# Decoder layer with retrieved experts: one sum kept in PSUM through the dense loop, gate loads of two rounds, and the second projection's first steps placed earlier

## The chip, the core and the metric

The kernel runs on one core of one Trainium2 chip. The number that counts is the device time of one execution in microseconds (us). The core has a matrix engine (TensorE, PE in the profile; its weight loads are listed as PEld), three engines for elementwise work (VectorE = DVE, ScalarE = ACT, GpSimd = POOL), and SyncE (SP), which here only starts DMA transfers. GpSimd also starts the indirect transfers that fetch table rows by index.

## What is computed

One decoder layer for 1024 tokens of width 1024, all in float32. The reference, cut to its spine:

```python
x   = layer_norm(x, ln_in)
p   = x @ w_in                          # 3592 columns, split into 8 parts
fox = causal attention, 8 heads x 64, logits + cumulative log forget gate
hgr = gated recurrence, 4 heads, state 128 x 128
x   = layer_norm(ALPHA * x + concat(fox, hgr) @ w_out, ln_mix)
# PEER: every token takes 8 heads x 16 = 128 of 16384 one-neuron experts
q   = x @ w_q
s   = scores of q against 2 x 128 sub-keys per head
idx, gates = top 16 of the pair sums per head, softmax
h   = gelu(x . u_tab[idx]) * gates
x   = layer_norm(ALPHA * x + sum_e h_e * v_tab[idx_e], ln_ffn)
```

## The kernel before

Tokens are worked in eight blocks of 128 and three groups: blocks 0 and 1 (group 0), 2 to 5 (group 1), 6 and 7 (group 2). Float32 products are made of three matmuls in a rounded format (`mm3`): each operand is split into `hi` (a rounded copy, by ScalarE) and `lo` (the rest, by one subtraction on VectorE or GpSimd), and hi·hi, hi·lo and lo·hi are added up in PSUM.

The stages, in the order of emission in `mixers`: input projection of group 0 (`project`, `project_cols`: 17 column tiles `m` of 128 columns, then row-wise parts), the two mixers of group 0 (`fox`, `hgrn`), `mix_out` with a layer norm, `select` (queries, scores, top 16), `select_tail` (pair sums, indices, gates; nearly all VectorE). Then the input projection of the other 768 tokens: `preload` loads their six normalised blocks from DRAM, `project` transposes them (48 transposes into `psf` banks, the hi and lo parts written to `xh`, `xl`; in every second block by a ScalarE copy `tsx` and a subtraction on GpSimd) and `project_cols` does the 17 column tiles at 768 columns. Then groups 1 and 2 follow in the same way without a further projection.

The experts are done in two ways. For blocks 0, 1, 6, 7 (`GATHER`) GpSimd fetches one expert row for each of 128 tokens at a time into one of eight row buffers (`rows`, 128x1024), and VectorE multiplies it with the tokens and sums (`gather_u`, L1124) or adds it, scaled, to the output (`gather_v`, L1149). These steps wait in queues (`ujobs`, `vjobs`) that `tick` draws on while other stages are emitted, by rates of each stage; after group 0, `HOLD = 7` ticks pass before the first. For blocks 2 to 5 (`DENSE`, 512 tokens) all 16384 experts are computed: `gbuild` writes the gates as a dense table `d_g` to DRAM, and `dense` loops over it.

`dense` has 32 rounds of four tiles of 128 experts. `up(g)` loads the round's gates `gt` (1 MB), and for each tile a 512-KB piece of u (`ur`), splits it, makes 24 matmuls into a `psh` bank, then gelu, gate product (L1047) and split. `down(g)` does the 1024 output columns in two halves of 512: per half four tiles of v (`vr`, 256 KB), four token blocks, three matmuls each, into four banks (three `psf`, one `psv`); after the half VectorE adds each bank to the sum `y` in SBUF (L1064, 128x512). PSUM holds two `psh`, one `psv` and three `psf` banks and one tile `y` of two banks (`psy`), which only `gather_v` of block 0 uses. `down` of a round runs beside `up` of the next, and the gather steps of the last blocks run all along. `finish` and `finish_dense` do the last layer norm; its two rows g, b are loaded once, at the start of the dense loop (`lnf`), into two buffers of their own.

Instructions are emitted in this order, and then a scheduler places them on each engine by estimated costs, so that work of a later stage may stand earlier. Every engine runs its own list in order. Nearly all loads are started by SP, in order.

Of the kernel before, what the change touches and what calls it, by code (L numbers as in the profile page):

```python
# [8 lines left out]
F32 = mybir.dt.float32  # L9
# [11 lines left out]
P = 128  # L21
# [18 lines left out]
HOLD = 7  # L40
# [7 lines left out]
GORD = (0, 1, 2, 3, 4, 5)  # L48
Q = {"qk": "a", "hs": "a"}
# [20 lines left out]
JG = 4  # L70


class Layer:
    def __init__(self, ctx, tc, a, out, dbg=None):
# [3 lines left out]
        self.ujobs, self.vjobs, self.bjobs, self.owed = [], [], [], [0.0] * 3  # L78
        self.nu = self.nv = 0
        self.hold = 0.0  # L80
        self.lnf = None
# [94 lines left out]
    def tick(self, phase, T=None, w=1.0):  # L176
        rate = RATE[phase] if T is None else RATE[phase][T]
# [145 lines left out]
    def mixers(self, groups, es):  # L323
        st, gb, tl = ExitStack(), ExitStack(), ExitStack()
# [5 lines left out]
        for n, (t0, T) in enumerate(groups):  # L330
# [32 lines left out]
            if n == 0:  # L363
                x1 = self.preload(T, S - T)
# [10 lines left out]
            if n == 0:  # L375
                x1 = self.project(T, S - T, st, x1)
                self.lx.close()
# [42 lines left out]
    def project(self, t0, T, st, xs=None):  # L420
        pa = st.enter_context(self.pool("pa", 1, "right"))
        xh = pa.tile([P, DC, T], F32R, name="xh", tag="xh")
        xl = pa.tile([P, DC, T], F32R, name="xl", tag="xl")

        def split(n, x):
            self.transpose_split("f", x, xh, xl, n)

        if t0:
            with self.pool("pt", 2, "right") as pt:
                for n, x in enumerate(xs):  # L430
                    self.transpose_split("f", x, xh, xl, n, pt if n % 2 < PSPL else None)
        else:
            pl = self.lx.enter_context(self.pool("pl", 2, "left"))
            self.first_ln(pl, 0, T, split)
            self.lns = [lambda r0=r0: self.first_ln(pl, r0, 2 * P, lambda n, x: None) for r0 in range(T, S, 2 * P)]
        return xh, xl

    def preload(self, t0, T):
        pl = self.lx.enter_context(self.pool("pl", 1, "left"))
        xs = []  # L440
        for n in range(T // P):
            x = pl.tile([P, D], F32, name="x", tag="x", bufs=T // P)
            self.q("x1l").dma_start(x, self.d_x1[t0 + n * P : t0 + (n + 1) * P])
            xs.append(x)
        return xs

    def project_cols(self, t0, T, xh, xl):
# [3 lines left out]
        with self.pool("pb", 2, "right") as pb:  # L451
            for m in range(17):
# [566 lines left out]
    def dense(self, prep, tail, tl):  # L1019
# [4 lines left out]
        with self.pool("dw", 2, "left") as dw, dws:  # L1024
# [9 lines left out]

            def up(g):
                gt = dw.tile([P, TD // 32, JG, 32], F32, name="gt", tag="gt")
                nc.sync.dma_start(gt, self.d_g[:, :, g * JG : (g + 1) * JG, :].rearrange("q j i t -> j q i t"))
                for c in range(JG):
# [8 lines left out]
                    nc.vector.tensor_tensor(h3, h3, gt[:, :, c], op=ALU.mult)  # L1047
# [3 lines left out]

            def down(g, hs):
# [15 lines left out]
            def late():  # L1068
# [3 lines left out]
                self.lnf = self.ffn_rows([dv[0].tile([P, D], F32, name=n, tag=n, bufs=1) for n in ("dlg", "dlb")])  # L1072
# [3 lines left out]
            for g in range(NG + 1):  # L1076
# [21 lines left out]
            self.finish_dense(dv[0], y, dv[1])  # L1098

    def rows(self):  # L1100
        return self.gp.tile([P, D], F32, name="rows", tag="rows", bufs=NROWS)
# [122 lines left out]
    def finish(self, y, r0):  # L1224
# [4 lines left out]
        g, b = self.lnf or self.ffn_rows([self.rows() for _ in range(2)])  # L1229
# [87 lines left out]
```

## Time and profile before

| | us |
|---|---|
| time, median of 3 runs (lowest, highest) | 3052.78 (3049.38, 3057.18) |
| the profiled execution | 3059.49 |
| its span, first to last instruction | 3057.6 |
| mean granted clock of the matrix engine, share of full speed | 0.921 |
| PE busy in the span | 2614.2 (85%) |
| DVE busy | 2667.8 (87%) |
| ACT, POOL busy | 1091.4 (36%), 1612.5 (53%) |
| DMA | 887.11 MB, mean 290 GB/s |

The stages from the span's start: projection of group 0 until 121 us, its mixers until 197, `mix_out` and layer norm until 235, selection until 302, the tail of the selection with the transposes of the other blocks until 346, the 768-column projection until 586, the rest of groups 1 and 2 until 1515, the dense loop until 3037, the last layer norm until the end. A busy share is a mean over stages that differ: which engine sets the time is read stage by stage. Every engine's list is in order, so an instruction that waits also holds all that stand behind it.

### The profile page before, as it was taken

Reading aid. Unit: us, or ns where it says so; the run is one execution under the profiler, and the core shown is the slowest. Engines: PE = TensorE matmul, PEld = TensorE weight load, DVE = VectorE, ACT = ScalarE, POOL = GpSimd, SP = SyncE. Lnnn points to the kernel's source line nnn. Section 1 sums busy time; section 2 is a strip of 40 time slices with the busy share of each in tenths; the row PEclk is TensorE's granted clock in tenths of the full one; section 3 lists DMA queues with packets and bytes.
Section 4 is the critical chain, followed back from the end, with each engine's and each line's share of the span. In section 5 each row is a group of like instructions: output and inputs, shape, how many; then the busy total and the mean of one; then the engine's idle time right before and its main releaser. Section 6 shows DMA issues by size and latency. Waiting matters only on the chain.

```text
span 3057.6 us, 45196 instructions
## 1 busy us (share of the span) xinstructions
PE 2614.2 (85%) x15865; PEld 2140.4 (70%) x15865; DVE 2667.8 (87%) x5555; ACT 1091.4 (36%) x2068; POOL 1612.5 (53%) x1216
## 2 busy tenths in 40 slices
PE   7778699877669768779578999899989999999995
PEld 6768589755567545568457878777768877877874
DVE  8658776588778998689898999899999999999998
ACT  4733222365312233677522323232223323223321
POOL 2344377655665645110156666565476665656652
PEclk9878899878889879889789999999999999999998
DMA  7632499855877867865589999999999999999994
GB/s 278 195 138 90 178 333 326 256 157 163 303 279 270 288 199 255 312 258 194 192 305 343 361 366 381 333 370 368 345 355 363 372 386 362 359 361 342 371 334 164
DMA packets 338660, 887.11 MB, mean 290 GB/s; under 512 B 29912, under 2 KB 124136, under 8 KB 336000
## 3 DMA queue, kind: packets, MB, share of 16 engines
q0 software_dynamic: 147456, 536.94, 48.3%
q1 hardware_dynamic: 185200, 338.38, 31.7%
q10 hardware_dynamic: 5776, 8.90, 0.8%
q8 instruction: 125, 2.05, 0.3%
q14 instruction: 103, 0.84, 0.1%
HBM read 821.67 MB, written 62.42 MB: 289 GB/s over the span
## 4 chain that ended last, share of the span: by engine, by line
PE 40%; DVE 37%; issue 9%; DMA 6%; ACT 4%; POOL 3%; SPq 0%; DVEq 0%; POOLq 0%; ACTq 0%
DVE ys L1149 7%; PE psf L294 6%; PE psf L295 6%; PE psf L293 5%; DVE rows L1124 5%; PE psh L293 5%; PE psh L295 5%; PE psh L294 5%; POOL rows L1105 2%; DMA rows<-in_u,gsel 1%; DVE tw L808 1%; DVE dy L1064 1%; PE psv L294 1%; PE psv L718 1%; PE psv L295 1%
## 5 line engine op out<-in xcount | busy, mean ns | idle before, releaser
L1105 POOL DMA_INDIRECT rows<-in_u,gsel x512 | 688.4, 1345 | 585.6 <-DVE rows L1124 368.8
L1105 POOL DMA_INDIRECT rows<-in_v,gsel x512 | 640.9, 1252 | 437.7 <-DVE ys L1149 271.2
L1124 DVE SCALAR_TENSOR_TENSOR rows<-rows,gx 128x1024 f32<-128x1024 f32 x512 | 635.6, 1291 | 36.6 <-DMA rows<-in_u,gsel 27.8
L1149 DVE SCALAR_TENSOR_TENSOR ys<-rows,sd,ys 128x1024 f32<-128x1024 f32 x381 | 491.2, 1289 | 0.6
L293 PE MATMUL psh<-dxh,uh 128*128 128x512 f32 x1024 | 403.0, 394 | 29.4 <-ACT uh L1031 16.6
L295 PE MATMUL psh<-dxh,ul 128*128 128x512 f32 x1024 | 401.1, 392 | 9.5 <-DVE ul L1032 9.4
L294 PE MATMUL psh<-dxl,uh 128*128 128x512 f32 x1024 | 400.6, 391 | 0.0
L294 PE MATMUL psf<-vl,hh 128*128 128x512 f32 x768 | 311.0, 405 | 42.2 <-DVE vl L1032 41.4
L1031 ACT ACTIVATE vh<-vr 128x512 fp32r<-128x512 f32 x256 | 161.8, 632 | 436.1 <-PE psv L295 396.1
L295 PE MATMUL psf<-vh,hl 128*128 128x512 f32 x768 | 306.4, 399 | 0.0
L293 PE MATMUL psf<-vh,hh 128*128 128x512 f32 x768 | 278.5, 395 | 10.7 <-DVE dy L1064 8.8
L1031 ACT ACTIVATE uh<-ur 128x1024 fp32r<-128x1024 f32 x128 | 135.8, 1062 | 405.1 <-PE psh L294 400.0
L293 PEld LDWEIGHTS psh<-dxh,uh 128*128 128x128 f32 x1024 | 193.6, 189 | 77.2 <-ACT hs L1045 20.4
L295 PEld LDWEIGHTS psh<-dxh,ul 128*128 128x128 f32 x1024 | 193.5, 189 | 50.4 <-DVE ul L1032 10.5
L294 PEld LDWEIGHTS psh<-dxl,uh 128*128 128x128 f32 x1024 | 193.5, 189 | 39.5
L294 PEld LDWEIGHTS psf<-vl,hh 128*128 128x128 f32 x768 | 148.1, 193 | 89.7 <-DVE vl L1032 59.0
L215 ACT ACTIVATE whi<-wraw 128x1024 fp32r<-128x1024 f32 x106 | 111.6, 1056 | 230.9 <-PE psf L294 64.8
L1032 DVE TENSOR_TENSOR vl<-vr,vh 128x512 fp32r<-128x512 f32 x256 | 170.7, 689 | 12.0 <-ACT vh L1031 11.9
L293 PEld LDWEIGHTS psf<-vh,hh 128*128 128x128 f32 x768 | 145.5, 190 | 48.1 <-DVE dy L1064 9.8
L218 DVE TENSOR_TENSOR wlo<-wraw,whi 128x1024 fp32r<-128x1024 f32 x60 | 81.8, 1365 | 100.8 <-ACT whi L215 98.0
L295 PEld LDWEIGHTS psf<-vh,hl 128*128 128x128 f32 x768 | 148.1, 193 | 29.8
L1032 DVE TENSOR_TENSOR ul<-ur,uh 128x1024 fp32r<-128x1024 f32 x128 | 156.6, 1224 | 11.5 <-ACT uh L1031 10.5
(342 smaller groups left out, 6156.5 us busy)
## 6 DMA issues: line engine op xcount, KB each, us to landing
ur<-in_ut SPq DMA_DIRECT2D x128, 512.0 KB
vr<-in_v SPq DMA_DIRECT2D x256, 256.0 KB
d_g<-slab SPq DMA_DIRECT2D x16, 2048.0 KB
gt<-d_g SPq DMA_DIRECT2D x32, 1024.0 KB
wraw<-in_wq SPq DMA_DIRECT2D x48, 512.0 KB
wraw<-in_wt SPq DMA_DIRECT2D x34, 512.0 KB
wraw<-in_wn SPq DMA_DIRECT2D x24, 512.0 KB
wraw<-in_wo SPq DMA_DIRECT2D x24, 512.0 KB
```

Source lines behind the costliest of these rows:

```text
L215: nc.scalar.activation(hi, raw, AF.Copy)
L218: eng.tensor_tensor(lo, raw, hi.bitcast(F32), op=ALU.subtract)
L293: mm(out, lh, rh, start=start, stop=False, **kw)
L294: mm(out, lh, rl, start=False, stop=False, **kw)
L295: mm(out, ll, rh, start=False, stop=stop, **kw)
L718: nc.tensor.matmul(pv[:, qb], ps[:, qb * P : (qb + 1) * P], V[:, kb], start=kb == 0, stop=kb == b0 + qb, skip_group_check=True)
L808: nc.vector.match_replace(w, out_v[:, 0:8], vals, FMIN)
L1031: nc.scalar.activation(hi, raw, AF.Copy)
L1032: nc.vector.tensor_tensor(lo, raw, hi.bitcast(F32), op=ALU.subtract)
L1105: self.nc.gpsimd.indirect_dma_start(out=t, out_offset=None, in_=tab, in_offset=bass.IndirectOffsetOnAxis(ap=idx, axis=0))
L1124: self.pin(nc.vector.scalar_tensor_tensor(u, u, 1.0, x2, op0=ALU.mult, op1=ALU.mult, accum_out=sd[:, n : n + 1]), "u")
L1149: self.pin(nc.vector.scalar_tensor_tensor(ys, v, h, ys, op0=ALU.mult, op1=ALU.add), "w")
```

## The change

Five parts. `down` keeps the sum of dense block 0 (`tb = 0`, token block 2) in the two banks of the `psy` tile through all 32 rounds, and adds it to `y` once, in the last; the other three blocks take `psf`, `psf`, `psf` in the first half and `psv`, `psf`, `psf` in the second. The gates of two rounds come with one load (`GT = 8`). `early` takes the place of `preload` and of the transposes in `project`: it is a sequence of steps that `tick` calls during the attention of group 0 (0.34 of a step at each of 18 ticks); six steps load and transpose one block each, into the `psy` tile, with ScalarE copies and VectorE subtractions; four more do the first four column tiles (`NEARLY = 4`) with raw, hi and lo in three of the `rows` buffers and the product in the `psy` tile; what is left is drained before `select_tail`. `project_cols` then begins at `m = 4`. `HOLD` becomes 3.5. And `lnf` is gone: each `finish` loads g and b into two `rows` buffers, `finish_dense` takes two `ur` buffers.

```diff
-HOLD = 7
+HOLD = 3.5
+NEARLY = 4
+ERATE = {"fox": 0.34, "hgrn": 0.0, "mix": 0.0, "sel": 0.0}
+GT = 8
...
     def tick(self, phase, T=None, w=1.0):
+        if self.ahead and phase in ERATE:
+            self.due += w * ERATE[phase]
+            while self.due >= 1.0:
+                self.due -= 1.0
+                next(self.ahead, None)
+            return
...
+            if n == 0:
+                pa = ex.enter_context(self.pool("pa", 1, "right"))
+                x1 = [pa.tile([P, DC, S - T], F32R, name=m, tag=m) for m in ("xh", "xl")]
+                self.ahead = self.early(T, S - T, *x1, pa)
...
-            if n == 0:
-                x1 = self.preload(T, S - T)
...
             if n == 0:
-                x1 = self.project(T, S - T, st, x1)
-                self.lx.close()
+                self.drain([self.ahead])
+                self.ahead = None
...
+    def early(self, t0, T, xh, xl, pa):
+        nc, a = self.nc, self.a
         for n in range(T // P):
+            x = self.rows()
             self.q("x1l").dma_start(x, self.d_x1[t0 + n * P : t0 + (n + 1) * P])
+            pt = self.psy.tile([P, D], F32, name="y", tag="y")
+            for c in range(DC):
+                nc.tensor.transpose(pt[:, c * P : (c + 1) * P], x[:, c * P : (c + 1) * P], self.ident)
+            sl = slice(n * P, (n + 1) * P)
+            for c0 in range(0, DC, 4):
+                v = pt[:, c0 * P : (c0 + 4) * P].rearrange("p (c t) -> p c t", c=4)
+                h = xh[:, c0 : c0 + 4, sl]
+                nc.scalar.activation(h, v, AF.Copy)
+                nc.vector.tensor_tensor(xl[:, c0 : c0 + 4, sl], v, h.bitcast(F32), op=ALU.subtract)
+            yield
+        for m in range(NEARLY):
+            raw, hi, lo = self.rows(), self.rows(F32R), self.rows(F32R)
+            self.q("w").dma_start(raw, a["wt"][m])
+            nc.scalar.activation(hi, raw, AF.Copy)
+            nc.vector.tensor_tensor(lo, raw, hi.bitcast(F32), op=ALU.subtract)
+            wh, wl = (t.rearrange("p (c m) -> p c m", c=DC) for t in (hi, lo))
+            po = self.psy.tile([P, D], F32, name="y", tag="y")
+            s = pa.tile([P, T], F32, name="es", tag="es", bufs=1)
+            for c0 in range(0, T, 512):
+                cs = slice(c0, min(c0 + 512, T))
+                for dc in range(DC):
+                    self.mm3(po[:, cs], wh[:, dc], wl[:, dc], xh[:, dc, cs], xl[:, dc, cs], dc == 0, dc == DC - 1)
+                nc.scalar.activation(s[:, cs], po[:, cs], AF.Copy, scale=0.125 if m < 4 else 1.0)
+            h = m % 4
+            self.q("qk").dma_start((self.d_q, self.d_k)[m // 4][h * P : (h + 1) * P, t0 : t0 + T], s)
+            yield
...
-            for m in range(17):
+            for m in range(NEARLY if t0 else 0, 17):
...
             def up(g):
-                gt = dw.tile([P, TD // 32, JG, 32], F32, name="gt", tag="gt")
-                nc.sync.dma_start(gt, self.d_g[:, :, g * JG : (g + 1) * JG, :].rearrange("q j i t -> j q i t"))
+                if g * JG % GT == 0:
+                    i0 = g * JG
+                    gts[0] = dw.tile([P, TD // 32, GT, 32], F32, name="gt", tag="gt")
+                    nc.sync.dma_start(gts[0], self.d_g[:, :, i0 : i0 + GT, :].rearrange("q j i t -> j q i t"))
+                gt = gts[0]
...
             def down(g, hs):
+                if g == 0:
+                    whole[0] = self.psy.tile([P, D], F32, name="y", tag="y")
                 for n in range(2):
-                    acc = [self.bank("f") for _ in range(ND - 1)] + [self.bank("v")]
+                    acc = [whole[0][:, ns]] + [self.bank("v" if n and tb == 1 else "f") for tb in range(1, ND)]
...
-                            self.mm3(acc[tb], hs[c][0][:, ts], hs[c][1][:, ts], vh, vl, c == 0, c == JG - 1)
+                            first, last = (g == 0, g == NG - 1) if tb == 0 else (True, True)
+                            self.mm3(acc[tb], hs[c][0][:, ts], hs[c][1][:, ts], vh, vl, first and c == 0,
+                                     last and c == JG - 1, skip_group_check=tb == 0)
...
-                    for tb in range(ND):
+                    for tb in range(0 if g == NG - 1 else 1, ND):
...
-                self.lnf = self.ffn_rows([dv[0].tile([P, D], F32, name=n, tag=n, bufs=1) for n in ("dlg", "dlb")])
+                    gb = self.ffn_rows([dw.tile([P, D], F32, name="ur", tag="ur", bufs=3) for _ in range(2)])
...
-        g, b = self.lnf or self.ffn_rows([self.rows() for _ in range(2)])
+        g, b = self.ffn_rows([self.rows() for _ in range(2)])
```

How the scheduler places it is seen on the engines' lists. The first place is PE around the layer norm of group 0: the end of `mix_out` (`psf<-whi,mh` and the like), the transposes of its result (`psf<-ident,res`) and the first queries of the selection (`psf<-mh,whi`). Before:

```order
L294 MATMUL psf<-wlo,mh 128x256
L295 MATMUL psf<-whi,ml 128x256
L275 MATMUL psf<-ident,res 128x128 x16
L293 MATMUL psf<-mh,whi 128x256
L294 MATMUL psf<-ml,whi 128x256
L295 MATMUL psf<-mh,wlo 128x256
```

After, from the last matmuls of column tile `m = 1` on (the rows that write `y` from `rows` are column tiles of `early`):

```order
L304 MATMUL y<-xh,rows 128x256
L302 MATMUL y<-xh,rows 128x256
L284 MATMUL psf<-ident,res 128x128 x8
L303 MATMUL y<-xl,rows 128x256
L304 MATMUL y<-xh,rows 128x256
L284 MATMUL psf<-ident,res 128x128 x4
L302 MATMUL y<-xh,rows 128x256
L303 MATMUL y<-xl,rows 128x256
L304 MATMUL y<-xh,rows 128x256
L284 MATMUL psf<-ident,res 128x128 x4
L302 MATMUL y<-xh,rows 128x512
L303 MATMUL y<-xl,rows 128x512
```

The second column tile now stands between `mix_out` and the queries, its end among the transposes, and the third (from `128x512` on) behind the transposes, ahead of the queries. The first tile, 48 matmuls, stands on PE right ahead of `mix_out`, and the fourth behind the last scores.

The second place is DVE at the end of the first selection tail, token block 1 (`oh`, `ij`, `eo`, `sel` belong to the tail, `wlo` to the column tiles). Before:

```order
L898 TENSOR_TENSOR ij<-oh 128x128
L218 TENSOR_TENSOR wlo<-wraw,whi 128x1024
L912 SCALAR_TENSOR_TENSOR eo<-ij 128x128
L872 CAST fi<-si 128x256
L893 TENSOR_TENSOR oh<-ab,i_3644 128x2048
L927 CAST sel<-eo 128x128
L895 TENSOR_TENSOR oh<-oh,fi 128x2048
L929 CAST sel<-psh 128x128
L897 TENSOR_TENSOR oh<-oh 128x1024
L930 COPY sel<-gt 128x128
L897 TENSOR_TENSOR oh<-oh 128x512
L218 TENSOR_TENSOR wlo<-wraw,whi 128x1024
```

After:

```order
L942 SCALAR_TENSOR_TENSOR eo<-ij 128x128
L227 TENSOR_TENSOR wlo<-wraw,whi 128x1024
L957 CAST sel<-eo 128x128
L959 CAST sel<-psh 128x128
L227 TENSOR_TENSOR wlo<-wraw,whi 128x1024
L1165 SCALAR_TENSOR_TENSOR rows,sd<-rows,gx_4201 128x1024 x3
L227 TENSOR_TENSOR wlo<-wraw,whi 128x1024
L1165 SCALAR_TENSOR_TENSOR rows,sd<-rows,gx_4201 128x1024 x5
```

The two subtractions `wlo` that stood inside the tail now stand behind its `eo`; the first of them is that of column tile `m = 5`, and the first gather steps (`rows,sd`) follow.

The third place is DVE late in the dense loop, the adds after the second half of one round and what stands among them (`ys` is a gather step, `hs`, `hl` belong to the next round's gates). Before:

```order
L1064 TENSOR_TENSOR dy_15614<-dy_15614,psf_23449 128x512
L1149 SCALAR_TENSOR_TENSOR ys_23529<-rows_23541,sd_16842,ys_23529 128x1024
L1064 TENSOR_TENSOR dy_15614<-dy_15614,psf_23450 128x512
L1149 SCALAR_TENSOR_TENSOR ys_23529<-rows_23544,sd_16842,ys_23529 128x1024
L1047 TENSOR_TENSOR hs_23628<-hs_23628,gt_23303 128x512
L1149 SCALAR_TENSOR_TENSOR ys_23529<-rows_23547,sd_16842,ys_23529 128x1024
L1049 TENSOR_TENSOR hl_23596<-hs_23628,hh_23595 128x512
L1149 SCALAR_TENSOR_TENSOR ys_23529<-rows_23550,sd_16842,ys_23529 128x1024
L1064 TENSOR_TENSOR dy_15614<-dy_15614,psf_23451 128x512
L1149 SCALAR_TENSOR_TENSOR ys_23529<-rows_23553,sd_16842,ys_23529 128x1024
L1064 TENSOR_TENSOR dy_15614<-dy_15614,psv_23452 128x512
```

After:

```order
L1105 TENSOR_TENSOR dy_15572<-dy_15572,psv_23312 128x512
L1190 SCALAR_TENSOR_TENSOR ys_23401<-rows_23410,sd_16870,ys_23401 128x1024
L1082 TENSOR_TENSOR hs_23500<-hs_23500,gt_23165 128x512
L1190 SCALAR_TENSOR_TENSOR ys_23401<-rows_23413,sd_16870,ys_23401 128x1024
L1084 TENSOR_TENSOR hl_23468<-hs_23500,hh_23467 128x512
L1190 SCALAR_TENSOR_TENSOR ys_23401<-rows_23416,sd_16870,ys_23401 128x1024
L1105 TENSOR_TENSOR dy_15572<-dy_15572,psf_23313 128x512
L1190 SCALAR_TENSOR_TENSOR ys_23401<-rows_23419,sd_16870,ys_23401 128x1024
L1105 TENSOR_TENSOR dy_15572<-dy_15572,psf_23314 128x512
```

Of four adds three are left, the first of them from the `psv` bank; the gather steps stand between them as before.

## Rows read from the trace of the kernel before

**Rows 1.** stretch, length, busy PE, PEld, DVE, ACT, POOL, clock, DMA share, GB/s.

```profile
121.00:197.00 76.00, 47.44 (x612) 38.44 (x610) 53.28 (x149) 37.63 (x105) 30.53 (x30) 0.65 0.46 153
302.00:346.00 44.00, 17.00 (x66) 12.54 (x67) 43.24 (x153) 13.78 (x25) 11.29 (x7) 0.65 0.16 54
346.00:586.00 240.00, 239.78 (x1651) 223.99 (x1650) 151.91 (x228) 59.43 (x82) 169.17 (x114) 1.00 0.90 319
1515.00:3037.00 1522.00, 1427.57 (x6110) 1153.41 (x6108) 1469.37 (x1999) 436.19 (x642) 928.35 (x691) 0.97 0.95 349
2400.00:2600.00 200.00, 195.05 (x843) 158.02 (x842) 197.82 (x259) 60.03 (x89) 123.46 (x97) 0.99 1.01 374
```

**Rows 2.** DVE's groups, dense loop: count; busy us, mean ns; idle before.

```profile
L1149 DVE SCALAR_TENSOR_TENSOR ys<-rows,sd,ys 128x1024 f32<-128x1024 f32 x381 | 491.2, 1289 | 0.6
L1124 DVE SCALAR_TENSOR_TENSOR rows<-rows,gx 128x1024 f32<-128x1024 f32 x312 | 364.1, 1222 | 10.9 <-DMA gx<-d_x 7.7 <-DMA rows<-in_u,gsel 3.2
...
L1064 DVE TENSOR_TENSOR dy<-dy,psf 128x512 f32<-128x512 f32 x192 | 126.4, 681 | 1.6 <-PE psf L295 1.6
...
L1064 DVE TENSOR_TENSOR dy<-dy,psv 128x512 f32<-128x512 f32 x63 | 43.0, 682 | 0.0
```

**Rows 3.** waits, dense loop: waiter, releaser, us in total, times, longest.

```profile
POOL rows L1105 <- DVE rows L1124: 320.4, 46, 184.1
POOL rows L1105 <- DVE ys L1149: 284.3, 287, 11.5
...
ACT vh L1031 <- DMA vr<-in_v: 16.0, 7, 3.7
```

**Rows 4.** PE's instructions in the dense loop: start us, us, form.

```profile
2302.34 0.39 PE L295 MATMUL psh<-dxh,ul 128*128 128x512 f32 x1
2302.57 0.39 PE L293 MATMUL psh<-dxh,uh 128*128 128x512 f32 x1
```

**Rows 5.** waits around one `finish` in the dense loop, 2195 to 2250 us.

```profile
POOL rows L1105 <- DVE rst L235: 7.6, 1, 7.6
```

**Rows 6.** PE's instructions, 189 to 346 us; in brackets idle before, releaser.

```profile
196.47 0.69 PE L741 MATMUL psf<-ident,o 128*128 128x128 f32 x2 [6.26 <-DVE o L736]
...
205.13 0.28 PE L294 MATMUL psf<-wlo,mh 128*128 128x256 f32 x1
205.25 0.28 PE L295 MATMUL psf<-whi,ml 128*128 128x256 f32 x1
...
230.42 3.65 PE L275 MATMUL psf<-ident,res 128*128 128x128 f32 x16 [8.33 <-DVE res L262]
...
335.17 0.80 PE L293 MATMUL psf<-xh,whi 128*128 128x512 f32 x1 [4.66 <-ACT whi L215]
```

**Rows 7.** the groups by form, 300 to 350 us.

```profile
L284 POOL TENSOR_TENSOR xl<-tsx,xh 128x512 fp32r<-128x512 f32 x6 | 8.7, 1461 | 33.3 <-ACT tsx L283 33.3
...
L286 DVE TENSOR_TENSOR xl<-psf,xh 128x512 fp32r<-128x512 f32 x6 | 3.8, 678 | 0.0
...
L218 DVE TENSOR_TENSOR wlo<-wraw,whi 128x1024 fp32r<-128x1024 f32 x2 | 2.4, 1221 | 0.0
```

**Rows 8.** DVE's instructions in the selection tail.

```profile
319.67 1.30 DVE L885 CAST plo<-psh 128x128 f32<-128x128 uint32 x1
...
330.32 0.23 DVE L885 CAST plo<-psh 128x128 f32<-128x128 uint32 x1
...
356.18 0.29 DVE L929 CAST sel<-psh 128x128 int32<-128x128 f32 x1 [0.16 <-PE psh L928]
```

**Rows 9.** DMA queues during a gate load, 1492 to 1496 us: packets, MB, share.

```profile
q1 hardware_dynamic: 1606, 0.82, 71.4%
```

**Rows 10.** DMA queues during 1-KB packets, 584 to 588 us.

```profile
q1 hardware_dynamic: 384, 0.38, 26.9%
```

**Rows 11.** SP around one gate load: start, us the queue was held.

```profile
2261.74 0.38 SPq L1037 DMA_DIRECT2D gt<-d_g  x1
2262.88 9.63 SPq L1030 DMA_DIRECT2D ur<-in_ut  x1
```

More of the change, by code (lines that the diff above doesn't have):

```diff
@@ L78, in __init__ @@
         self.ujobs, self.vjobs, self.bjobs, self.owed = [], [], [], [0.0] * 3
+        self.ahead, self.due = None, 0.0
         self.nu = self.nv = 0
         self.hold = 0.0
-        self.lnf = None
         PS = bass.MemoryType.PSUM
@@ L323, in mixers @@
     def mixers(self, groups, es):
[L324 removed]
+        st, gb, tl, ex = ExitStack(), ExitStack(), ExitStack(), ExitStack()
         self.lx = ExitStack()
@@ L337, in mixers @@
                 tl.close()
+            ex.close()
+            if n == 0:
+                pa = ex.enter_context(self.pool("pa", 1, "right"))
+                x1 = [pa.tile([P, DC, S - T], F32R, name=m, tag=m) for m in ("xh", "xl")]
+                self.ahead = self.early(T, S - T, *x1, pa)
             po = st.enter_context(self.pool("po", 1, "left"))
@@ L426, in split @@
             self.transpose_split("f", x, xh, xl, n)
[L428 to L435, printed above, removed]
+        pl = self.lx.enter_context(self.pool("pl", 2, "left"))
@@ L436, in project @@
+        self.first_ln(pl, 0, T, split)
+        self.lns = [lambda r0=r0: self.first_ln(pl, r0, 2 * P, lambda n, x: None) for r0 in range(T, S, 2 * P)]
         return xh, xl
-    def preload(self, t0, T):
-        pl = self.lx.enter_context(self.pool("pl", 1, "left"))
-        xs = []
+    def early(self, t0, T, xh, xl, pa):
+        nc, a = self.nc, self.a
         for n in range(T // P):
-            x = pl.tile([P, D], F32, name="x", tag="x", bufs=T // P)
+            x = self.rows()
             self.q("x1l").dma_start(x, self.d_x1[t0 + n * P : t0 + (n + 1) * P])
-            xs.append(x)
-        return xs
+            pt = self.psy.tile([P, D], F32, name="y", tag="y")
[24 more added lines that the diff above has]
+            yield
@@ L1050, in up @@
                     yield hh, hl
+            whole = [None]
             def down(g, hs):
+                if g == 0:
+                    whole[0] = self.psy.tile([P, D], F32, name="y", tag="y")
                 for n in range(2):
                     ns = slice(n * 512, (n + 1) * 512)
-                    acc = [self.bank("f") for _ in range(ND - 1)] + [self.bank("v")]
+                    acc = [whole[0][:, ns]] + [self.bank("v" if n and tb == 1 else "f") for tb in range(1, ND)]
                     for c in range(JG):
@@ L1095, in dense, with rows @@
                     dv[1] = dv[0].tile([P, ND, 2, 6], F32, name="lnst", tag="lnst", bufs=1)
+                    gb = self.ffn_rows([dw.tile([P, D], F32, name="ur", tag="ur", bufs=3) for _ in range(2)])
                 if h:
                     prev = down(g, h)
-            self.finish_dense(dv[0], y, dv[1])
-    def rows(self):
-        return self.gp.tile([P, D], F32, name="rows", tag="rows", bufs=NROWS)
+            self.finish_dense(dv[0], y, dv[1], gb)
+    def rows(self, dt=F32):
+        return self.gp.tile([P, D], dt, name="rows", tag="rows", bufs=NROWS)
     def gather_rows(self, tab, idx):
@@ L1200, in gather_v, with finish_dense @@
         self.finish(ys, r0)
-    def finish_dense(self, pool, y, st):
+    def finish_dense(self, pool, y, st, gb):
         nc, V = self.nc, self.nc.vector
-        g, b = self.lnf
+        g, b = gb
         mv = pool.tile([P, ND, 2], F32, name="lnmv", tag="lnmv")
```

3 lines of the change are left out of this document (2 added, 1 removed).

## The prediction

> **What bounds the kernel now.** I read the page's 40 slices first: DMA and VectorE stand at 9 from the middle of the span to its end, with two weaker stretches before. Then the busy time by stage [rows 1]. In the dense loop (1522 us, half of the time) VectorE is busy 1469.4 us, 96.5%, DMA 95%, PE 1427.6 us, 94%: three candidates close together. What tells them apart are the waits [rows 3]: the gather's fetches on GpSimd wait 320.4 + 284.3 us for VectorE to give a row buffer back, while VectorE waits for fetched rows 3.2 us in all and for PE's banks 1.6 [rows 2]. So VectorE paces the gathers, and since it works one list in order, it paces the splits and the dense rounds between them too. PE needs less than it shows: matmuls of 512 columns start 0.227 us apart [rows 4], and 32 rounds hold 4 × 24 up and 2 × 4 × 4 × 3 down, 6144 in all, 1395 us. DMA has its ring full because buffers come free at VectorE's pace, but at 0.95 it isn't far behind.
>
> Before the dense loop two stretches matter. In 121 to 197 us (mixers of group 0) PE works 47.4 of 76.0 us, VectorE 53.3, ScalarE 37.6: there is room. In 302 to 346 VectorE is full (43.2 of 44.0, the selection's tail) and PE works 17.0; its last transposes and first column tile, from 335.17 us on [rows 6], wait for what that tail lets through. From 346 to 586 PE is solid, 239.8 of 240.0 us at the full clock [rows 1]: whatever column work leaves this stretch shortens it, if its new place has room.
>
> **The dense sum.** Per round 8 adds become 6, and the last has 8: 62 of 256 adds of 0.682 us go [rows 2], 42.3 us of VectorE. No wait for a free bank comes with it: PE adds on in the two banks, and per half it needs three fresh banks in place of four. Against that, the earlier start of the gathers at `HOLD` 3.5 is by tiles, not by time: projection begins at `m = 4` and the order shows the first fetches at `m = 7` (before at 6), with 4 steps of gather left over for the loop, 4 × 1.29 = 5.2 us [rows 2]. VectorE's work there goes to 1469.4 − 42.3 + 5.2 = 1432.3; at the same 96.5% the loop is 1484 us, −38. But PE's 1395 us are then 94% of it and DMA's share is near full, and each of the three waits now and then for another. I take −28 (bounds −42, all of the adds, and −10, if most of it turns into waits).
>
> **g and b.** Three of the four `finish` calls formerly took loaded rows; now each loads two (512 KB each, into 2 of 8 row buffers) while the fetches wait. One `finish` already stops them for 7.6 us, since its sum holds a buffer [rows 5]. VectorE has other work in its list meanwhile, splits and adds. I take +3 for the three (0 to +10). `finish_dense` finds its rows loaded a round before: 0; not hidden, it would be two loads' landing, some 10 us, within the range.
>
> **Gates.** Sixteen loads of 2 MB in 1024-B pieces for 32 of 1 MB in 512-B pieces. During a gate load 1606 packets took 71.4% of 16 engines for 4 us, 28.5 ns each [rows 9]; 1-KB packets elsewhere took 0.269 × 64 / 384 = 44.8 ns [rows 10], though among other kinds. Two for one saves 2 × 28.5 − 44.8 = 12 ns, of 32768 pairs over 16 engines: 25 us of DMA time. It counts 0 in the sum, since VectorE ends last, not DMA. The Trainium skill (DMA: Bandwidth & Descriptors, Specifications) gives 512 B as the least transfer for line rate; by that the 512-B pieces were already at it and nothing is saved, against 28.5 and 44.8 ns in the rows; the sum is the same by either, and only the DMA rival below would lose its 25 us.
>
> **Transposes and column tiles.** Six blocks are transposed during group 0's mixers: 48 transposes at 0.228 us each (16 took 3.65 us [rows 6]), 10.9 us of PE; 12 subtractions of 0.678 us and 4 `wlo` of 1.22 [rows 7], 13 us of VectorE, before 6 and none. The stretch has 28.6 us of PE and 22.7 of VectorE unused, but the chain through softmax and recurrence is in order on the same lists, so part is felt: +8 (0 to +13). Tile `m = 0` stands ahead of `mix_out`: 24 matmuls at 0.227 and 24 of 256 columns at 0.12 [rows 4, 6] are 8.3 us, over the 6.26 us PE idles there: +2. Tile 1 lies in the layer norm's gap of 8.33 us [rows 6]: 0 to +1. Tile 2 stands ahead of the queries, 8.3 us in full, less about 1.3 because PE no longer idles before the queries (the granted clock is 0.65 of full in the two stretches with gaps, 1.00 in the solid one [rows 1]; 1.3 is my choice): +7. Tile 3 stands behind the last scores, where PE waits for the tail anyway: 0. The selection so ends 17 us later.
>
> The tail is then lighter: 6 subtractions of 0.678 (3.8 us) and two `wlo` of 1.22 (2.4) are gone from it, as the order shows. And small VectorE steps that take 0.23 us alone took 1.2 to 1.3 while GpSimd did its subtractions of 1461 ns [rows 7, 8]; there were six of those, and they are gone: 4 us more. Together −10; the tail, which ends at 356.5 [rows 8], ends at about 363, and PE is free of it some 5 us earlier, since `m = 4` goes ahead of its end. What is left of projection then: of 17 tiles at 24 × 0.227 + 24 × 0.12 = 8.35 us four are gone, 33.4 us, of which 4.4 us had been done before 346 in the kernel before: 240 − 29 = 211, less half of tile 4 (about 5) that runs beside the tail, 206 us. From about 362 it ends at 568, for 586: −18. Bounds: −36, if the earlier stretches hide all; +5, if the added 17 us double and the tail gains nothing.
>
> **Sum.** −28 − 18 + 3 = −43 us against the profiled execution, 3059.5 (its span 3057.6 and 1.9 around it): 3016.5. That execution lies 6.7 over the median of the runs, 3052.8; so 3010.
>
> **The rivals.** A: DMA paces the dense loop. Its share is 0.95, 1446 us of 1522 [rows 1]. It would lose 25 and gain ten transfers of 0.52 MB (6 more rows of g and b, 4 fetches), at the 374 GB/s of 2400 to 2600 us [rows 1] 14 us: 1435, at the same share 1511, −11. With −18 + 3 this is −26: 3027. For it: share 1.01 in that stretch; against: VectorE is at 99% there too and does not wait for rows. Chance 0.12. By the Trainium skill's 512 B, named above, the 25 us would be lost and this case be the loop +15 and the sum 0, 3053.
>
> B: the early steps cost what they save. Order on PE is fixed: if tiles 0 and 2 and the steps in the mixers stand in front of work that paces the front, the selection ends 35 us later instead of 17, and projection ends where it did. For it: tile 2 stands in full ahead of the queries; against: PE is idle a third of the mixers. Then −28 + 3: 3028. Chance 0.13.
>
> C, slower: the double gate load starves the loop. SP starts loads in order; the load behind a 1-MB gate load held the queue 9.63 us [rows 11], behind 2 MB it could be 19.3. The v pieces behind it go in five buffers, one used every 1522 / 256 = 5.9 us, 30 us ahead; ScalarE already waits 16.0 us for them [rows 3]. If each of 16 loads made PE wait 5 us past what its buffers cover, that is 80 us, less the 43: 3090. It turns the whole change slower from 43 / 16 = 2.7 us each. For it: those waits; against: 16 loads, not 32, and 20 us of cover behind even the long one. Chance 0.09.
>
> **The numbers.** Forecast 0.66, its own range 2982 (−42 and −28, toward the good ends) to 3033 (−10, −18, +8); A 0.12, B 0.13, C 0.09. A measurement of this kernel tells about 0.3%, 9 us, from no change. Faster: forecast nearly all, A and B for the most part, 0.85; within 9 us: the high ends of A and B, 0.07; slower: C and a little of B with C's waits, 0.08. The range 2984 to 3046 holds the forecast but its edge, A and B, and leaves C out.
>
> **What will show it.** The dense loop, from the first gate product to the last add: 1490 to 1500 us, with 194 adds (160 `psf`, 32 `psv`, 2 `y`); 1511 with DMA at 0.95 or more and VectorE under 95% is A. The mixers of group 0: 84 us for 76. PE solid in the columns from about 360 and done at 568; at 586 it is B. Small VectorE steps of 1.2 us gone from the tail. Waits of ScalarE for `vr` near 16 us; several times that, behind the gate loads, is C. I am wrong in kind if VectorE is no more the engine that others wait for in the dense loop, and in size if the mixers stretch by more than 13 us.

## The result: slower by half a per cent

The changed kernel takes 3071.3 us in the median of 8 runs (3065.9 to 3078.8), the kernel before 3055.9 on the same chip (8 runs, 3049.4 to 3063.2): a ratio of 1.0053, interval 1.0036 to 1.0069. The forecast was 3010 with a range of 2984 to 3046, so it was wrong in sign and outside its range. The profiled execution of the changed kernel has a span of 3076.8 us.

Where the time went is seen from four marks in the two profiles. The columns of the 768-token projection end at 559.4 us, 28 us earlier than before (587.5). The first up-matmul of the dense loop starts at 1498.9, only 5 us earlier (1504.1): 23 us are lost on the way. And the loop, from the first up-matmul to the last add, takes 1572.4 us for 1548.0: 24 us more, though 62 adds are gone.

The stages of the changed kernel, with the columns of [rows 1]; 346 to 560 is its solid projection, 1499 to 3071 its loop:

```profile
121.00:197.00 76.00, 56.48 (x696) 46.56 (x695) 55.02 (x166) 46.46 (x123) 23.42 (x26) 0.80 0.33 105
197.00:235.00 38.00, 34.81 (x262) 32.61 (x261) 15.78 (x32) 12.31 (x15) 17.55 (x8) 1.00 0.37 119
302.00:346.00 44.00, 27.27 (x124) 21.72 (x122) 43.55 (x213) 7.39 (x15) 3.43 (x1) 0.82 0.20 72
346.00:560.00 214.00, 208.01 (x1461) 194.84 (x1461) 145.58 (x217) 51.25 (x69) 160.55 (x109) 0.97 0.91 334
1499.00:3071.00 1572.00, 1435.01 (x6146) 1164.86 (x6146) 1458.51 (x1975) 442.31 (x648) 950.36 (x696) 0.96 0.93 342
```

The mixers of group 0 take in 9 us more of PE work in the same 76 us. The loop before, between the same two marks (those of [rows 1] leave its edges out):

```profile
1504.00:3052.00 1548.00, 1438.45 (x6146) 1161.81 (x6146) 1487.64 (x2031) 442.49 (x649) 931.61 (x692) 0.97 0.94 345
```

So VectorE is now busy 92.8% of the loop for 96.1%, PE 91.3% for 92.9%, DMA 0.93 for 0.94: nobody is closer to full, all three wait more. VectorE's groups there, for [rows 2]:

```profile
L1165 DVE SCALAR_TENSOR_TENSOR rows<-rows,gx 128x1024 f32<-128x1024 f32 x316 | 369.2, 1221 | 13.5 <-DMA rows<-in_u,gsel 13.3
...
L1105 DVE TENSOR_TENSOR dy<-dy,psf 128x512 f32<-128x512 f32 x160 | 105.6, 679 | 0.0
...
L1105 DVE TENSOR_TENSOR dy<-dy,psv 128x512 f32<-128x512 f32 x32 | 21.8, 680 | 0.0
...
L1105 DVE TENSOR_TENSOR dy<-dy,y 128x512 f32<-128x512 f32 x2 | 1.4, 685 | 1.0 <-PE y L304 1.0
```

160, 32 and 2 adds at 0.68 us, as worked out; 42 us of VectorE are really gone. The waits of the loop, for [rows 3]:

```profile
POOL rows L1146 <- DVE rows L1165: 318.6, 48, 174.0
POOL rows L1146 <- DVE ys L1190: 269.5, 269, 10.3
...
ACT uh L1061 <- DMA ur<-in_ut: 44.2, 5, 14.2
...
ACT vh L1061 <- DMA vr<-in_v: 19.2, 4, 7.7
```

New is the third row: ScalarE waits 44.2 us for pieces of u, up to 14.2 at a time. In the kernel before it waited so once in the whole loop:

```profile
ACT uh L1031 <- DMA ur<-in_ut: 5.2, 1, 5.2
```

The front, for [rows 6]: tile 0 of `early`, one matmul of `mix_out`, the transposes after the layer norm, the first tile of `project_cols`:

```profile
185.90 0.78 PE L302 MATMUL y<-xh,rows 128*128 128x512 f32 x1
...
198.85 0.28 PE L302 MATMUL psf<-whi,mh 128*128 128x256 f32 x1
...
230.12 1.06 PE L284 MATMUL psf<-ident,res 128*128 128x128 f32 x8
...
329.60 0.60 PE L302 MATMUL psf<-xh,whi 128*128 128x512 f32 x1 [2.61 <-ACT whi L224]
```

Tile 0 starts at 185.9, before the last head is done, and fills the idle time of 6.26 us that stood there. From 185.9 to 197.4 us PE is busy 10.81 of 11.50 us, before 3.70, and `mix_out` runs from its first matmuls at the high clock (granted 1.00 of full from 197 to 235 us, 0.12 us a matmul); before, its first 20 took 0.21 us each. It ends at 221.8 us, before at 222.1. The tail of the selection, for [rows 8]:

```profile
329.50 0.22 DVE L915 CAST plo<-psh 128x128 f32<-128x128 uint32 x1
...
342.72 0.22 DVE L915 CAST plo<-psh 128x128 f32<-128x128 uint32 x1
...
352.56 0.28 DVE L959 CAST sel<-psh 128x128 int32<-128x128 f32 x1
```

Both CASTs that stood at 1.30 and 0.23 us now take 0.22, and the tail ends at 352.8, 3.6 us earlier than before, not 6 later.

### The profile page after: what moved, and what is told of

It is laid out like the page before. It is cut to its first block, busy times and chain, and to the rows that moved or that the text cites. A ratio compares the mean times of both kernels' runs of the same rounds, so it can differ in the third digit from the quotient of the medians.

```text
span 3076.8 us, 44996 instructions
## 1 busy us (share of the span) xinstructions
PE 2617.9 (85%) x15865; PEld 2147.9 (70%) x15865; DVE 2624.9 (85%) x5500; ACT 1087.5 (35%) x2061; POOL 1611.7 (52%) x1209
## 4 chain that ended last, share of the span: by engine, by line
PE 43%; DVE 28%; DMA 10%; issue 10%; ACT 5%; POOL 4%; SPq 0%; POOLq 0%; DVEq 0%; ACTq 0%
PE psf L303 5%; DVE ys L1190 5%; PE psf L304 5%; PE psf L302 5%; PE psh L304 5%; PE psh L302 5%; PE psh L303 5%; DVE rows L1165 4%; DMA ur<-in_ut 3%; POOL rows L1146 3%; DMA rows<-in_v,gsel 2%; PE psv L748 2%; PE y L303 2%; DMA rows<-in_u,gsel 1%; PE psf L711 1%
## 5 line engine op out<-in xcount | busy, mean ns | idle before, releaser
L302 PE MATMUL psh<-dxh,uh 128*128 128x512 f32 x1024 | 403.5, 394 | 34.8 <-ACT uh L1061 20.5
L302 PE MATMUL psf<-vh,hh 128*128 128x512 f32 x640 | 239.7, 397 | 28.3 <-DVE dy L1105 28.2
L303 PE MATMUL psf<-vl,hh 128*128 128x512 f32 x640 | 253.9, 397 | 0.0
L304 PE MATMUL psf<-vh,hl 128*128 128x512 f32 x640 | 253.3, 396 | 0.0
L227 POOL TENSOR_TENSOR wlo<-wraw,whi 128x1024 fp32r<-128x1024 f32 x45 | 111.5, 2482 | 128.4 <-ACT whi L224 127.8
L302 PEld LDWEIGHTS psf<-vh,hh 128*128 128x128 f32 x640 | 121.5, 190 | 60.4 <-DVE dy L1105 35.5
L303 PE MATMUL y<-vl,hh 128*128 128x512 f32 x256 | 106.0, 414 | 47.2 <-DVE vl L1062 47.0
L304 PEld LDWEIGHTS psf<-vh,hl 128*128 128x128 f32 x640 | 122.8, 192 | 26.4
```

Source lines behind the costliest of these rows:

```text
L227: eng.tensor_tensor(lo, raw, hi.bitcast(F32), op=ALU.subtract)
L302: mm(out, lh, rh, start=start, stop=False, **kw)
L303: mm(out, lh, rl, start=False, stop=False, **kw)
L304: mm(out, ll, rh, start=False, stop=stop, **kw)
```

## The experiments

Each ratio is to the kernel before on the same chip, with its interval. Chips differ by up to 18 us in the median and by 11 in the time until the loop, so profiles of different chips are compared with that care. A profile is one execution, too: those of e3 and e4 lie 9 and 10 us below the medians of their runs, that of e2 7 above. The marks of all profiles, in us:

| run | columns end | first step of gate table | first up-matmul | loop | ratio |
|---|---|---|---|---|---|
| before | 587.5 | 1234.1 | 1504.1 | 1548.0 | 1 |
| changed | 559.4 | 1223.4 | 1498.9 | 1572.4 | 1.0053 |
| e1 sum only | 587.4 | 1247.6 | 1515.6 | 1528.6 | 0.9948 |
| e2 front only | 559.0 | 1254.1 | 1523.8 | 1572.6 | 1.0072 |
| e3 gates of one round | 558.6 | 1246.0 | 1515.9 | 1532.0 | 0.9970 |
| e4 and g, b once | 561.3 | 1245.8 | 1515.8 | 1525.3 | 0.9955 |
| e5 before again | 588.5 | 1238.2 | 1504.9 | 1554.4 | 1 |
| e6 front, credit | 557.1 | 1194.5 | 1467.7 | 1568.7 | 0.9999 |
| e7 as e4, credit | 562.3 | 1201.5 | 1477.0 | 1530.9 | 0.9883 |
| e8 changed, gates spread | 560.9 | 1221.2 | 1496.7 | 1537.7 | 0.9951 |
| e9 changed, credit | 560.5 | 1202.7 | 1481.4 | 1566.4 | 0.9973 |
| e10 changed, credit, spread | 563.4 | 1208.0 | 1488.0 | 1534.4 | 0.9894 |
| e11 front, credit, HOLD 7 | 560.4 | 1193.0 | 1469.7 | 1576.4 | 0.9980 |
| e12 g, b in row buffers | 587.3 | 1234.4 | 1504.5 | 1567.9 | 1.0045 |

e1 to e4 ran on one chip, e5 to e8 on a second, e9 to e12 on a third.

**e1, the sum alone.** The kernel before with the change's `down`:

```diff
...
-                    acc = [self.bank("f") for _ in range(ND - 1)] + [self.bank("v")]
+                    acc = [whole[0][:, ns]] + [self.bank("v" if n and tb == 1 else "f") for tb in range(1, ND)]
...
-                    for tb in range(ND):
+                    for tb in range(0 if g == NG - 1 else 1, ND):
```

> The kernel before with one edit: the sum of dense block 0 stays in the two PSUM banks. The dense loop is taken from the first up-matmul to the last add into y: 1548 us before, 1572 after the whole change. Theory 'feeds' (the sum itself pays; the double gate load and the g and b rows in finish cost more than it gives): loop 1520 to 1535, time 3028 to 3043. Rival 'sum' (the accumulated sum is what makes the loop longer): loop 1555 or more, time 3063 or more. Rival 'floor' (VectorE does not set the loop's time, the matmuls do at 43.6 us a round, so 62 adds less change nothing): loop 1543 to 1550, time 3050 to 3058.

3055.5 us, ratio 0.9948 (0.9930 to 0.9966). The absolute numbers expected were for the first chip; against its own chip's 3073.9 this is −16 us, the loop 1528.6. "Feeds" holds in kind, "sum" and "floor" fall. But 42.3 us of VectorE give 16, not 28.

Where they give nothing is seen round by round (a round is counted from its first gelu to that of the next; the first is round 0). Rounds 16 to 19 fetch rows of u only, rounds 9 to 13 and 21 to 30 rows of v only; the three stretches in the order of time, in the kernel before, then in e1, columns as in [rows 1]:

```profile
1937.32:2168.29 230.97, 223.47 (x966) 181.72 (x967) 226.69 (x252) 67.88 (x101) 137.28 (x109) 0.99 0.99 366
2271.15:2448.49 177.34, 176.66 (x770) 143.37 (x770) 174.19 (x281) 54.33 (x82) 119.82 (x86) 1.00 1.00 370
2492.53:2966.11 473.58, 453.93 (x1944) 367.61 (x1945) 465.45 (x525) 138.77 (x205) 287.47 (x221) 0.98 0.98 358
```

```profile
1941.40:2173.23 231.83, 227.32 (x985) 186.58 (x986) 227.09 (x249) 69.32 (x105) 152.75 (x114) 0.99 1.01 377
2279.78:2456.15 176.37, 176.23 (x769) 142.84 (x767) 172.80 (x279) 54.35 (x82) 120.73 (x87) 1.00 1.01 378
2507.70:2958.77 451.07, 440.47 (x1922) 361.13 (x1921) 445.12 (x496) 137.30 (x203) 292.79 (x218) 0.99 1.00 370
```

In the rounds of u PE was busy 176.66 of 177.34 us already, and eight adds fewer give 1 us. In the fifteen rounds of v PE had 27 us to spare, and thirty adds fewer, 20.5 us of VectorE, give 21.6 (704.5 to 682.9), all of it in the last ten, since work also shifts between rounds. This is one profile each, on two chips.

**e2, the front alone.** The changed kernel without its edits to `down`, `up` and `lnf`:

```diff
-GT = 8
+GT = 4
...
-                    acc = [whole[0][:, ns]] + [self.bank("v" if n and tb == 1 else "f") for tb in range(1, ND)]
+                    acc = [self.bank("f") for _ in range(ND - 1)] + [self.bank("v")]
...
-                    gb = self.ffn_rows([dw.tile([P, D], F32, name="ur", tag="ur", bufs=3) for _ in range(2)])
```

> The changed kernel with the dense loop put back as it was (four adds, gates of one round, g and b loaded once): only the early transposes and tiles and HOLD 3.5 are left. All theories: columns end near 559 us for 587 before. Theory 'given back' (the 28 us are lost again before the dense loop, where the table of gates sets the pace): first up-matmul at 1499 for 1504, time 3047 to 3053. Rival 'passed on' (the loss before the loop in the changed kernel came from something in the dense part's placing): first up-matmul near 1476, time 3025 to 3032. Rival 'front hurts the loop' (4 fetches more and later): time 3058 or more.

1.0072 (1.0057 to 1.0088), +22 us. The columns end at 559.0, and the loop starts at 1523.8, 8 later than with the front of before on this chip (e1). So the 28 us are given back before the loop, and the loop is longer too.

**e3, gates of one round; e4, g and b loaded once as well.**

```diff
-GT = 8
+GT = 4
...
+                self.lnf = self.ffn_rows([dv[0].tile([P, D], F32, name=n, tag=n, bufs=1) for n in ("dlg", "dlb")])
...
-        g, b = self.ffn_rows([self.rows() for _ in range(2)])
+        g, b = self.lnf or self.ffn_rows([self.rows() for _ in range(2)])
```

> The changed kernel with gates of one round per load again (GT 4); sum in PSUM, g and b in row buffers, and early steps stay. Theory 'feeds': the waits of ScalarE for ur and vr behind the gate loads (44 and 19 us in the loop) go back to some 16, the loop to 1545 to 1560, time 3045 to 3060; the stop of about 17 us at the finish of the second gather block stays. Rival 'g and b alone': loop 1568 to 1575, time 3066 to 3074.

> As the run before it, and g and b loaded once at the start of the loop as in the kernel before: what is left of the change is the sum and the early steps. Theory 'feeds': 12 to 20 us less than with g and b in row buffers, loop 1520 to 1540, time 3020 to 3040. Rival 'floor': as the front alone, 3047 to 3053. Rival 'sum': 3060 or more.

e3: 0.9970 (0.9955 to 0.9984); e4: 0.9955 (0.9940 to 0.9971). The double load is worth 1.0053 / 0.9970, 0.83% or 25 us; the rows of g and b 0.15%, 5 us, within the intervals. e4 has the sum and the front, and is no better than the sum alone (0.9948). So "feeds" holds for the gates: in e3 ScalarE waits 0.2 us for pieces of u, for 44.2, and the loop takes 1532.0. For g and b it asked 12 to 20 us and missed.

**Where the front's time went.** The loop can start when the tail of group 1's selection and the table of gates (64 steps) are done. They are emitted by `tick` from a third queue, and each phase adds to that queue's credit, `owed[2]`, also while the queue is empty, up to 16. In the kernel before, the ticks of group 0's mixers fill it to 16 and it waits there for group 2, when the queue first has work. In the changed kernel these ticks `return` early for `early`, and the credit starts at 0: 16 credits at 2 a step are 8 steps. On VectorE's list 29 steps of the table have been begun ahead of the layer norm behind group 2's `mix_out` (its first `lnmv`) in the kernel before, 21 in the changed one and 29 again in e9. Five runs (e6, e7, e9 to e11) set the credit by one line:

```diff
                 self.ahead = None
+                self.owed[2] = 16.0
```

**e5, the kernel before again**, for a profile on the second chip.

> The kernel before itself, for a profile on the chip of these runs, since chips differ: on the chip of the first four experiments its median was 18 us higher. All theories: dense loop (first up-matmul to last add) 1545 to 1560 us, first up-matmul between 1500 and 1520.

Its single profiled run took 3066.9 us, ten over the 3056.8 of that chip's 15 runs; the loop starts at 1504.9 and takes 1554.4.

**e6, the front with the credit; e7, sum and front with the credit.**

> The front part alone (early transposes and tiles, HOLD 3.5), with one line more: after the early steps are drained, the credit of the third queue (the tail of group 1 and the table of gates) is set to 16, the cap at which it stood in the kernel before; there the ticks of group 0's mixers filled it, in the changed kernel these ticks return early. Theory 'credit' (the front's 28 us are lost since the table of gates is placed 8 of its 64 steps later): gate table starts about 20 us earlier than with the front alone, first up-matmul 18 to 28 us earlier than there, ratio to before 0.997 to 1.003 (the front alone was 1.0072). Rival 'pace' (the table can't go faster whatever its place, because its slabs wait for their writes to DRAM): first up-matmul within 6 us of the front alone, ratio 1.005 to 1.009.

> Sum in PSUM and front part, gates of one round, g and b loaded once, and the credit set to 16. Theory 'credit': 18 to 28 us less than without the credit, ratio 0.986 to 0.990 (without it 0.9955). Rival 'pace': 0.994 to 0.997.

e6: 0.9999 (0.9987 to 1.0011); e7: 0.9883 (0.9868 to 0.9898), 3018.0 us and the fastest of all. "Credit" holds in both: 0.73% and 0.72% less, 22 us. "Pace" falls.

**e8, the gates of two rounds in eight pieces.**

```diff
-                    i0 = g * JG
-                    gts[0] = dw.tile([P, TD // 32, GT, 32], F32, name="gt", tag="gt")
-                    nc.sync.dma_start(gts[0], self.d_g[:, :, i0 : i0 + GT, :].rearrange("q j i t -> j q i t"))
+                    gts[0] = gts[1]
                 gt = gts[0]
                 for c in range(JG):
+                    k = (g * JG + c) % GT
+                    i1 = g * JG + c - k + GT
+                    if i1 < P:
+                        if k == 0:
+                            fresh()
+                        nq = TD // 32 // GT
+                        gates(i1, k * nq, (k + 1) * nq)
```

Here `fresh` takes the next buffer and `gates` loads one piece of the next two rounds' gates into it.

> The changed kernel, its gates still of two rounds in 1024-byte pieces, but the next pair's table is loaded in eight pieces of 256 KB, one ahead of each tile of experts, in place of one load of 2 MB. Theory 'burst' (the loss of the double load comes from u and v pieces that wait behind 2 MB on SP's queue and in the DMA rings): the waits of ScalarE for ur and vr fall from 63 to under 25 us, ratio 0.994 to 0.999 (the changed kernel 1.0053, with one-round loads 0.997). Rival 'size' (1024-byte pieces or the buffers cost the same wherever they are issued): 1.003 to 1.007.

0.9951 (0.9937 to 0.9964): "burst" holds, "size" falls. Same bytes, same pieces of 1024, same buffers, and 1.0% less. ScalarE's waits for transfers of u and v fall from 63 to 35 us, not under the 25 expected; those for pieces of u fall from 44.2 to 0.9.

**e9 and e10, the changed kernel with the credit, without and with the spread.**

> The changed kernel with one line more: the credit of the third queue set to 16 after the early steps, nothing else. Theory 'credit': first up-matmul 18 to 30 us earlier than in the changed kernel (1499), ratio to before 0.996 to 1.000 (the changed kernel 1.0053). Rival 'tied to the rest' (the credit helped only with the loads of one round): ratio 1.003 to 1.006.

> The changed kernel with the credit and the gates of two rounds in eight pieces a tile ahead. If the two losses add: 0.9951 - 0.0073 = 0.988, the same as sum and front with one-round gates and the credit (0.9883). If they overlap (the loop takes back what the front gives): 0.992 to 0.995.

e9: 0.9973 (0.9956 to 0.9989), e10: 0.9894 (0.9876 to 0.9912). With one line the change turns from slower to faster, and "tied to the rest" falls. The two losses add, as near as the intervals tell: the credit is worth 0.57% with the spread (e8 to e10) and 0.80% without, the spread 0.79% with the credit. What the credit does, in the first step of the gate table on VectorE, in the kernel before, the changed one and e9:

```profile
1234.12 0.69 DVE L962 TENSOR_TENSOR ohi<-iota16h,gpair 128x1024 f16<-128x1024 f16 x1
```

```profile
1223.44 0.69 DVE L992 TENSOR_TENSOR ohi<-iota16h,gpair 128x1024 f16<-128x1024 f16 x1 [2.08 <-ACT gpair L985]
```

```profile
1202.69 0.69 DVE L993 TENSOR_TENSOR ohi<-iota16h,gpair 128x1024 f16<-128x1024 f16 x1
```

And the stretch from the start of group 2's mixers to that step, columns as in [rows 1], in the same order:

```profile
1060.00:1234.00 174.00, 125.39 (x1365) 83.62 (x1365) 152.89 (x630) 66.95 (x186) 86.99 (x87) 0.84 0.72 241
```

```profile
1031.00:1223.00 192.00, 138.04 (x1494) 93.74 (x1494) 155.70 (x634) 71.93 (x203) 93.59 (x98) 0.85 0.74 243
```

```profile
1029.00:1203.00 174.00, 125.64 (x1367) 82.60 (x1365) 153.31 (x631) 66.94 (x186) 86.30 (x86) 0.86 0.71 234
```

The mixers start 29 us earlier in the changed kernel. But its table begins 129 matmuls later in PE's list (1494 for 1365), and the stretch takes 192 us for 174, VectorE idle 36 for 21. With the credit it is 174 again with 1367 matmuls.

What the gate load does is seen in round 10 of e9 and of e10, which differ in the gates alone. The stretch, and ScalarE's and PE's waits in it; first e9, whose 2-MB load was issued 9 us before:

```profile
1964.00:2020.00 56.00, 47.82 (x204) 39.14 (x203) 45.87 (x50) 14.79 (x22) 28.16 (x24) 0.94 0.92 329
```

```profile
ACT uh L1062 <- DMA ur<-in_ut: 13.4, 1, 13.4
...
PE y L303 <- DVE vl L1063: 8.2, 1, 8.2
```

```profile
GB/s 399 403 378 384 397 395 396 413 398 408 411 394 414 398 394 183 60 25 240 236 241 341 394 411 277 372 366 398 334 310 196 298 306 370 322 255 288 240 344 389
```

Then e10:

```profile
1969.00:2015.00 46.00, 46.00 (x205) 38.09 (x204) 45.96 (x50) 14.98 (x22) 28.65 (x24) 1.00 1.03 403
```

```profile
ACT vh L1062 <- DMA vr<-in_v: 2.9, 1, 2.9
```

```profile
GB/s 427 409 417 415 399 408 391 400 384 393 393 416 401 388 397 391 404 399 403 402 410 403 403 395 406 392 399 426 411 402 406 410 406 406 410 410 397 403 408 383
```

The GB/s rows are 40 slices of the stretch. In e9 the transfers run at about 400 GB/s for 20 us, the piece of u behind the gates lands late, ScalarE waits 13.4 us for it and PE for the split behind that; meanwhile the transfers fall to 60 and 25 GB/s. In e10 as many bytes (18.5 MB) flow at 383 to 427 GB/s without a break and PE is busy 46.0 of 46.0. By rounds, e9 loses 10.2, 5.9 and 8.4 us in rounds 10, 12 and 28 against e10, together 24 of the loop's 32; most other gate loads cost nothing. SP's queue itself was held no longer than before, 9.44 us for the 9.63 in [rows 11]; here in the changed kernel, ahead of its round 10:

```profile
1972.56 0.38 SPq L1071 DMA_DIRECT2D gt<-d_g  x1
1973.20 9.44 SPq L1060 DMA_DIRECT2D vr<-in_v  x2
```

The prediction's 25 us of DMA time from larger pieces are mostly there, without a gain in the kernel's time. The queue of SP's loads over all of e3 (gates in pieces of 512 B), then over all of e8 (1024 B): packets, MB, share of 16 engines' span:

```profile
q1 hardware_dynamic: 186064, 341.53, 32.2%
```

```profile
q1 hardware_dynamic: 154720, 341.53, 31.7%
```

That is 983 us of 3053.4 and 964 of 3039.9 for the same bytes, 19 less (966 in the changed kernel, too). But e8, 0.9951, is not clear of e3, 0.9970: the intervals overlap, and the chips differ. The Trainium skill (DMA: Bandwidth & Descriptors, Specifications) gives 512 B as the least transfer for line rate, by which larger pieces would save nothing. The packets' times do not bear that out, the kernel's time shows no saving either way, and the measurement decides.

**e11, HOLD 7.**

```diff
-HOLD = 3.5
+HOLD = 7
```

> The front alone with the credit, but HOLD 7 as in the kernel before. With HOLD 3.5 the first up-matmul came 37 us earlier in the profiles and the median was the same (0.9999), since the dense loop was 14 us longer in its profile. Theory 'phase' (the loop is longer because the gather stands 4 steps off against the rounds): loop back to 1550 to 1556, ratio 0.990 to 0.994. Rival 'not HOLD': loop 1564 to 1572, ratio 0.998 to 1.002.

0.9980 (0.9963 to 0.9997), loop 1576.4: "phase" falls, "not HOLD" holds. So the front alone gains nothing to speak of even with its credit (e6, e11), while with the sum in PSUM it keeps 20 us (e7 against e1). In e6's profile the loop starts 37 us earlier than in e5 and is 14 us longer: two rounds are 24 longer (3 and 20, 65.5 and 57.0 us for 54.4 and 44.2; in 20 the gather goes over from u to v), the others 10 shorter. PE waits 36 us there for a bank that VectorE has still to add, for 13 in e5; with the sum in PSUM these waits are 21 us in e7 and 18 in e1. That execution was the fastest of e6's 11, 3043.7 for a median of 3055.5, so another 12 us show only in the median. Why the loop with four adds takes the front's gain back, and why these waits grow, stays open; no run isolates it.

**e12, g and b in row buffers.**

```diff
-                self.lnf = self.ffn_rows([dv[0].tile([P, D], F32, name=n, tag=n, bufs=1) for n in ("dlg", "dlb")])
...
-        g, b = self.lnf or self.ffn_rows([self.rows() for _ in range(2)])
+        g, b = self.ffn_rows([self.rows() for _ in range(2)])
```

> The kernel before with one edit: g and b are not loaded once, each finish loads them into two row buffers, and finish_dense into two u buffers. By the prediction's term: +3 us, 1.000 to 1.002. By the difference of the runs with one-round gates (0.9970 with, 0.9955 without): +5 us, 1.0015. Rival 'stop' (the first finish in the loop holds VectorE's list 12 to 17 us, as in the changed kernel): 1.004 to 1.006.

1.0045 (1.0028 to 1.0061), +14 us; "stop" has the size. Its place was not as said: round 15, with the finish, is only 2.2 us longer than in e5, round 20 is 10.4. In the changed kernel round 15 is the long one (69.2 us for 52.5), where VectorE waits for fetched rows and PE for ScalarE's gelu:

```profile
DVE rows L1165 <- DMA rows<-in_u,gsel: 10.1, 9, 2.9
...
PE psh L302 <- ACT hs L1080: 8.4, 1, 8.4
```

Little of that is g and b: round 15 takes 63.0 us in e1 and 59.6 in e4, which both load them once, and 66.8 in e3, 7.2 more than in e4.

## Why the prediction was wrong, step by step

From the kernel before to the changed one there is a path of runs, each a single step: the sum (e1) −16 us, the front with its credit (e1 to e7) −20, the credit lost (e7 to e4) +22, g and b in row buffers (e4 to e3) +5, the double gate load (e3 to the changed kernel) +25: +16, the measured difference. The steps are ratios times 3056, each uncertain by some 7 us; that they add up is no check, since each begins where the last one ends. In another order single ones would differ: g and b are 14 in e12, and the front with its credit is nothing without the sum (e6).

- **What bounds the loop: half right.** VectorE is the engine that GpSimd waits for, and fewer adds help. But the argument "VectorE ends last" was read from an average. In the kernel before, 13 rounds took under 45 us, nine of them with u fetches, beside the 43.6 that their 192 matmuls need at 0.227 us. There the sum gains nothing (e1: 1 us in rounds 16 to 19), and in the fifteen rounds of v it gains what the adds cost (21.6 us for 20.5); the other rounds together come out 4 us longer. So the term of −28 was mis-sized: −16. Nor did it come without a wait for a free bank: PE waits 28.2 us for VectorE's adds in the changed loop, 17.6 in e1, 14.2 before.
- **Gates: the step that failed.** "It counts 0 in the sum, since VectorE ends last, not DMA" took the load for volume. It is a burst. Rival C had the mechanism, pieces late behind 2 MB, though it named those of v alone, and asked 2.7 us a load to turn the change slower; it cost 25 / 16 = 1.6 on average, in three rounds most of it. It was given 0.09, on the grounds that 20 us of cover lay behind the load. That cover was counted for v, which has five buffers; u has three, and ScalarE's longest wait for a transfer in the loop, 14.2 us, was for a piece of u.
- **The missing step.** "The order shows" was used for where the early tiles stand, never for what the early `return` in `tick` leaves undone. It held the table of gates back by 8 steps: +22 to 24 us in the three pairs of runs without the spread, +17 with it. It was in the diff, and on VectorE's list: 21 steps for 29. No rival had it.
- **Transposes and tiles: right, even low.** −18 forecast, −28 at the end of the columns, −20 kept once credit and sum are there. The mixers did not grow (+8 forecast), tile 0 cost nothing (+2), the selection's last query matmul ended 10 us later, not 17, and the tail ended 3.6 earlier. Rival B falls.
- **g and b:** +3 in a range to +10; 5 in the changed kernel, 14 alone.
- **Rival A**, DMA as the pace: falls; its share of the loop went down, 0.93 for 0.94, though single rounds wait for transfers.

Without these two losses the kernel takes 3018 us (e7) or a ratio of 0.9894 (e10, all five parts kept): the forecast of 3010 was one of what the change could do, not of what it did.

## What to carry over

Read in a diff not only what new code issues but what an early return no longer does: counters, credits and queue states that later stages live on, and compare the order there too. A load that is made twice as large and half as often has the same volume and twice the burst; look for the smallest cover among all the loads behind it in its queue, or cut it in pieces a step ahead. And before a gain is put down to the busiest engine, take the time of each round: rounds that already stand at another engine's floor gave nothing here.

## What was not expected of the chip

A full stretch of 46 us at 403 GB/s with PE busy throughout (e10), against a mean of 342 in the changed kernel's loop. The Trainium skill (DMA: Bandwidth & Descriptors, Specifications) gives about 358 GB/s as the limit for one core, half of what two share; this run, on one core alone, is above it, and the measurement decides. And the same code reached the loop 11 us later on one chip than on another (e1 against the kernel before, whose lists are equal up to there); nearly all of it arises between 1070 and 1180 us, and why stays open.
